# Final state products of three head groups made inside the second norm, with their operands parked in DRAM

## The chip, the cores and the metric

The kernel runs on one core of a Trainium2 chip. The core has a matrix engine (PE, with its weight loads shown as PEld), a vector engine (DVE), an activation engine (ACT), a general engine (POOL) and a queue engine (SP) that here only issues transfers. Matrix products read SBUF and write to PSUM; POOL works on SBUF tiles. The metric is device time in microseconds for one execution of the whole program. Three runs of the kernel before gave 1777.72, 1773.81 and 1773.94 us, a median of 1773.94 us.

## The reference

One inference step of a decoder layer with 256 prompt tokens and 8 x 8 sample tokens (320 columns together), all in float32. The layer has a mixing part and a feed-forward part, each between two root-mean-square norms:

```
h = rms_norm(x);  proj = h @ w_in            # u, v | z | x, B, C | dt
mix = concat(chunk_gate(u, v), ssd(z, x, B, C, dt)) @ w_out
x = x + rms_norm(mix)                        # the "second norm"
f = gelu(g) * u of causal_conv(rms_norm(x) @ w_up);  x = x + rms_norm(f @ w_down)
```

The part the change touches is the state-space mixer (SSD). It has 32 heads in 4 groups of 8 heads; a group shares B and C. The prompt is cut in two chunks of 128 tokens. For a group, the state after the prompt is

```
states[c]  = B[c]^T (decay[c] * dt * x)[c]               # 128 x 512 for a group, one per chunk c
final      = chunk_decay * states[0] + states[1]         # returned as ssm_state_prompt
```

`states[0]` is needed for the outputs of the second chunk. `states[1]` is needed by nothing but `final`, which is only an output.

## The kernel before

Activations are kept transposed: features on the 128 partitions, 320 tokens along the free axis. Each large float32 product with weights is made from three reduced-precision products: weights and activations are split in a rounded high part and a remainder (`whi`, `wlo` and `h_hi`, `h_lo`), and high x high, high x low and low x high are accumulated (lines 153 to 155). Weights come in slabs of 128 x 1024 elements: SP loads `wraw`, ACT casts it to `whi` (L124), DVE subtracts to get `wlo` (L125), with three buffers of each.

The order of work is traced by Python code, and a planner then places each instruction: on each engine it takes, of the instructions that are ready in its own estimate, the one of highest priority; the priority is the place in the trace unless a block raises it (`first()` and `high_priority`). Tiles of one tag share a fixed number of buffers, and a new tile waits until an old one's last reader is done. `issue_after(ins)` orders those instructions of a block that run on the engine of `ins` behind `ins` in that engine's queue; instructions of the block on other engines are not ordered by it. Background tasks are Python generators in the list `bg`; the projection loops call `tick()` between slabs, which advances the first task by one step.

The mixer's second half runs four tasks `ssd(g)`, one per head group, while projections and output products fill PE. In a group: `xt_ps` transposes of x; `xdt` = dt * x; `x0d` = the decayed first chunk (POOL, L851, tag `xde`, two buffers); `s1_ps` = the product for `states[0]` (L897), copied by ACT to `s1` (L899, one buffer); the states of the samples (`up_ps`, `yo_ps`); decays of each head (`cs`, three buffers); the output products `y_ps` (L1004). At the end of the group `x1d`, the decayed second chunk (L851 again), is ready, POOL multiplies `s1` by the chunk decay (L1027), and `final()` (L1030 to L1036) makes the product `fin_ps` of `btok` and `x1d` (L1032), DVE adds it to `s1` (L1034), and a queue stores the result (L1035). For groups 0 to 2 this happens in the task itself after two more steps. For group 3 `final()` is kept in `rest` and its two halves are run in the second norm.

The second norm ends the mixing part. Its order is written out by hand: after the last output product, the last sample states of group 3 (`rest[0]`), the column sums of squares on PE (`tsum`, L294), the product `fin_ps` of group 3, the root (ACT, L282, recorded in `rooted`) and a Newton step on DVE (L283 to L286), then `spread` (L302), three PE transposes that leave 1/rms of every token in a PSUM bank, `r2b`. DVE reads that bank for the scaled residual (`x1_ready`: L1141, L1142), ACT makes the high part of the next norm's input (L401), DVE the low part (L402; its instruction is recorded in `low`), and the up projection starts. PE has no work of its own between `tsum` and the first product of the up projection. `idle_products` (L817) puts products there whose result nobody reads: one ahead of `spread` and seven behind it.

PSUM has eight banks: four of tag `mm` for projections and four of tag `ms` for everything else (`misc`). The first part of the up projection uses four `mm` banks and two `ms` banks; `r2b` holds a third `ms` bank until its last reader.

Of the kernel before, what the change touches and what calls it, by code (L numbers as in the profile page):

```python
# [9 lines left out]
F32 = mybir.dt.float32  # L10
# [3 lines left out]
ALU = mybir.AluOpType  # L14
# [3 lines left out]
P = 128  # L18
# [3 lines left out]
NT = NP + NS  # L22
# [12 lines left out]
def hybrid_step(  # L35
# [10 lines left out]
    act, dve, pool, pe, sp = nc.scalar, nc.vector, nc.gpsimd, nc.tensor, nc.sync  # L46
# [4 lines left out]
    dr = ctx.enter_context(tc.tile_pool(name="dr", bufs=1, space=DRAM))  # L51
# [5 lines left out]
    def misc(name):  # L57
        return ms.tile([P, 512], F32, tag="ms", name=name)
# [6 lines left out]
    with tc.high_priority(offset=300000):  # L65
        dve.memset(ones, 1.0)

        ps = misc("early")
# [202 lines left out]
    rsqrt_ins, sums_ins, spread_ins, rooted, low = [], [], [], [], []  # L271
# [17 lines left out]
    def token_sums(*sqs):  # L289

        ps = misc("tsum")
        for c, o in enumerate((0, P, NT - P)):
            for i, sq in enumerate(sqs):
                ins = pe.matmul(ps[:, c:c + 1], sq[:, o:o + P], ones[:, 0:1], start=i == 0, stop=i == len(sqs) - 1).ins  # L294
        sums_ins.append(ins)
        return ps[:, 0:3]
# [40 lines left out]
    def squares_of(total):  # L337

        one, held = [], []

        def step(nb):
            if nb < KD - 3:
                add_square(total, acc[:, nb, :], nb == 0)
                if nb == 0:

                    act.activation(tp.tile([P, 1], F32, name="root_there", bufs=1), total[:, 0:1], AF.Sqrt)
                return
            with first():
                if nb < KD - 1:
                    held.append(misc("sq_ps")[:, :NT])  # L350
                else:
                    one.append(tp.tile([P, NT], F32, tag="sq", name="sq", bufs=2))
                for ts in parts_of(nb):
                    act.activation((one or held)[-1][:, ts], acc[:, nb, ts], AF.Square)
                if nb > KD - 3:
                    dve.tensor_tensor(out=total, in0=total, in1=held.pop(0), op=ALU.add)
        return step, one


    dacs_d = dr.tile([NH, NT + NS], F32, name="dacs_d")  # L360
    tot_d = dr.tile([NH, NB], F32, name="tot_d")
    ssq_d = [dr.tile([P, NT // 32], F32, name=f"ssq_d{i}") for i in range(4)]


# [56 lines left out]
    with ExitStack() as mctx:  # L421
        op = mctx.enter_context(tc.tile_pool(name="op", bufs=1))
# [365 lines left out]
        with tc.tile_pool(name="sd", bufs=1) as sd:  # L788
# [23 lines left out]
            x_of = {0: x0}  # L812
            rest = []

            def idle_products(ps, n):
                for _ in range(n):
                    ins = pe.matmul(ps, bsp[:, 0, :P], bsp[:, 0, :], start=True, stop=True).ins  # L817
                return ins

            def ssd(g):  # L820

                xs = x_of[g]
# [125 lines left out]
                def end(i, by=act):  # L948
                    made = grown(sts[i], bms.pop(i))
                    store_state(i, sts[i], by)  # L950
                    return made
# [75 lines left out]
                pool.tensor_tensor(out=by_head(s1), in0=by_head(s1),  # L1027
                                   in1=dec[:, 2, h0:h0 + 8].unsqueeze(2).to_broadcast([P, 8, 64]), op=ALU.mult)

                def final():  # L1030
                    ps = misc("fin_ps")
                    made = pe.matmul(ps, btok[:, 1, bs], x1d, start=True, stop=True)  # L1032
                    yield made.ins
                    dve.tensor_tensor(out=s1, in0=s1, in1=ps, op=ALU.add)  # L1034
                    (pool if g == 3 else act).dma_start(o_ssm_p[g], s1)  # L1035
                    yield  # L1036
                if g == 3:
                    rest.extend([lambda: end(3, pool), final()])
                else:
                    yield  # L1040
                    yield
                    for _ in final():
                        pass

            tasks = [ssd(g) for g in range(4)]
            res = [[] for _ in range(4)]
# [50 lines left out]
            finish(norm3)  # L1097
            sq2 = hp.tile([P, NT], F32, tag="ssq", name="sq2")

            squares, one = squares_of(sq2)  # L1100
            chunk_out(w_out, 7, *res[3], False, squares, apart=True)

# [4 lines left out]
            with first():  # L1107
                with tc.issue_after(pd_last[-1]), tc.issue_after(added_last[0]):
                    made = rest[0]()
                with tc.issue_after(made):  # L1110
                    most = token_sums(sq2)
                with tc.issue_after(sums_ins[-1]):
                    ps = token_sums(*one)
                with tc.issue_after(sums_ins[-1]):
                    made = next(rest[1])
                r = rsqrt_by_root(most, ps, 1.0 / D)
                behind = rsqrt_ins[-1]

                idle = misc("idle")
                with tc.issue_after(made):  # L1120
                    made = idle_products(idle, 1)
                with tc.issue_after(made):
                    r2b = spread(r)
                with tc.issue_after(spread_ins[-1]):
                    idle_products(idle, 7)
            sq3 = hp.tile([P, NT], F32, tag="ssq", name="sq3")


# [18 lines left out]
            load_x(1)  # L1147
            up0 = []
            project(ffn_w_up, 0, None, late=up0, ready=x1_ready, after=behind, ahead=1, more=DFF, held=added)
            with tc.issue_after(low[2]):  # L1150
                next(rest[1])

            room = [op.tile([P, 4, NT], F32, tag="xs", name="sq_two", bufs=2) for _ in range(2)]
            total, *some = [t[:, i:i + 2, :] for t in room for i in (0, 2)]
# [281 lines left out]
```

## Time and profile before

| | |
|---|---|
| three runs | 1777.72, 1773.81, 1773.94 us; median 1773.94 us |
| profiled execution | 1774.69 us; span on the core 1773.0 us |
| granted TensorE clock | 0.999 of full |
| busy: PE, DVE, ACT, POOL | 1765.1, 1173.7, 817.9, 274.5 us |
| DMA | 290.01 MB, mean 164 GB/s |

The span is the time from the first to the last instruction of the core; 1.7 us of the execution lie outside it. A row of a timeline gives start, duration, engine, line, operation and operands, in us from the span's start; a bracket at its end gives the engine's idle time before it and what released it. The view of waits gives total, number and longest. A group's row gives shortest, median and longest duration in ns. The chain of work that ended last is followed back from the last instruction, so its pieces do not overlap and a piece on it is time that the program took.

### The profile page before, as it was taken

The numbers are of one execution on the slowest core, as the hardware profiler recorded it, in microseconds if no ns is written. First come the engines' busy times: TensorE is split into PE (matmuls) and PEld (weight loads), VectorE is DVE, ScalarE is ACT, GpSimd is POOL, SyncE is SP. The second block draws the span as 40 slices with busy tenths as digits, with TensorE's granted clock in tenths as the row PEclk, the third lists the DMA queues.
The fourth block names the chain that finished last, engine by engine and source line by source line (L and its number), as shares of the span: only waits on it lengthen the run. The fifth ranks groups of instructions, "written<-read, shape, count | busy, mean of one in ns | idle before, by whom it ended". The sixth has DMA issues, their size and how long they took to land.

```text
span 1773.0 us, 30633 instructions
## 1 busy us (share of the span) xinstructions
PE 1765.1 (100%) x11897; PEld 1711.9 (97%) x11897; DVE 1173.7 (66%) x2015; ACT 817.9 (46%) x1193; POOL 274.5 (15%) x602
## 2 busy tenths in 40 slices
PE   9999999999999999999999999999999999999998
PEld 7789999999999998999999999999999999999998
DVE  7549764657978778678865465656657575656575
ACT  5434555334564556445645334343434343333445
POOL 1202200000331313103211011010102010101004
PEclk9999999999999999999999999999999999999999
DMA  7556645455666666555554554555455544454542
GB/s 261 161 150 171 189 141 159 153 152 182 223 189 195 186 203 188 147 179 158 171 158 147 154 153 148 155 148 153 150 151 158 144 156 145 156 155 145 155 151 102
DMA packets 217297, 290.01 MB, mean 164 GB/s; under 512 B 19264, under 2 KB 146624, under 8 KB 216960
## 3 DMA queue, kind: packets, MB, share of 16 engines
q1 hardware_dynamic: 205424, 268.84, 50.1%
q10 hardware_dynamic: 10016, 14.16, 2.2%
q0 software_dynamic: 1712, 5.05, 1.0%
q8 instruction: 94, 1.54, 0.4%
q14 instruction: 51, 0.42, 0.1%
HBM read 273.17 MB, written 14.84 MB: 162 GB/s over the span
## 4 chain that ended last, share of the span: by engine, by line
PE 98%; DVE 1%; issue 0%; ACT 0%; ACTq 0%; DVEq 0%
PE ps L153 19%; PE ps L154 19%; PE ps L155 19%; PE pd L153 10%; PE pd L155 10%; PE pd L154 10%; PE ps_v L144 7%; PE y_ps L1004 1%; PE up_ps L925 0%; PE sg L752 0%; PE yo_ps L908 0%; PE xt_ps L414 0%; PE early L70 0%; PE x1p L1299 0%; DVE xsp L863 0%
## 5 line engine op out<-in xcount | busy, mean ns | idle before, releaser
L125 DVE TENSOR_TENSOR wlo<-wraw,whi 128x1024 fp32r<-128x1024 f32 (+1 forms) x476 | 582.3, 1223 | 421.4 <-ACT whi L124 419.6
L124 ACT CAST whi<-wraw 128x1024 fp32r<-128x1024 f32 (+1 forms) x475 | 495.1, 1042 | 714.5 <-PE ps L154 381.5
L153 PE MATMUL ps<-h_hi,whi 128*128 128x320 f32 x2268 | 700.6, 309 | 0.0
L154 PE MATMUL ps<-h_lo,whi 128*128 128x320 f32 x2268 | 699.3, 308 | 0.0
L155 PE MATMUL ps<-h_hi,wlo 128*128 128x320 f32 x2268 | 698.9, 309 | 0.0
L153 PEld LDWEIGHTS ps<-h_hi,whi 128*128 128x128 f32 x2268 | 425.7, 188 | 2.5 <-issue 1.6
L154 PEld LDWEIGHTS ps<-h_lo,whi 128*128 128x128 f32 x2268 | 425.8, 188 | 0.7
L155 PEld LDWEIGHTS ps<-h_hi,wlo 128*128 128x128 f32 x2268 | 425.6, 188 | 0.0
L155 PE MATMUL pd<-fhi,wlo 128*128 128x320 f32 x704 | 217.0, 308 | 0.0
L153 PE MATMUL pd<-fhi,whi 128*128 128x320 f32 x704 | 217.0, 308 | 0.0
L154 PE MATMUL pd<-flo,whi 128*128 128x320 f32 x704 | 217.0, 308 | 0.0
L153 PE MATMUL pd<-ohi,whi 128*128 128x320 f32 x448 | 139.1, 310 | 0.0
L155 PE MATMUL pd<-ohi,wlo 128*128 128x320 f32 x448 | 138.4, 309 | 0.0
L154 PE MATMUL pd<-olo,whi 128*128 128x320 f32 x448 | 138.1, 308 | 0.0
L153 PEld LDWEIGHTS pd<-fhi,whi 128*128 128x128 f32 x704 | 132.2, 188 | 0.0
L154 PEld LDWEIGHTS pd<-flo,whi 128*128 128x128 f32 x704 | 132.2, 188 | 0.0
L155 PEld LDWEIGHTS pd<-fhi,wlo 128*128 128x128 f32 x704 | 132.2, 188 | 0.0
L1201 POOL COPY ptf<-pad 128x2 f32<-128x2 f32 x88 | 21.0, 238 | 602.7 <-DVE pad L1189 601.9
L249 DVE TENSOR_TENSOR acc_ffn<-acc_ffn,pd 128x320 f32<-128x320 f32 (+1 forms) x161 | 77.5, 482 | 37.8 <-PE pd L155 36.3
L153 PEld LDWEIGHTS pd<-ohi,whi 128*128 128x128 f32 x448 | 84.1, 188 | 1.6 <-issue 1.0
L154 PEld LDWEIGHTS pd<-olo,whi 128*128 128x128 f32 x448 | 84.1, 188 | 0.3
L155 PEld LDWEIGHTS pd<-ohi,wlo 128*128 128x128 f32 x448 | 84.1, 188 | 0.2 <-issue 0.2
(335 smaller groups left out, 1866.5 us busy)
## 6 DMA issues: line engine op xcount, KB each, us to landing
wraw<-in_ffn_w_up SPq DMA_DIRECT2D x176, 512.0 KB, 3.6
wraw<-in_w_in SPq DMA_DIRECT2D x140, 512.0 KB, 3.8
wraw<-in_ffn_w_down SPq DMA_DIRECT2D x88, 512.0 KB, 3.3
wraw<-in_w_out SPq DMA_DIRECT2D x64, 512.0 KB, 3.4
st<-in_state_ssm SPq DMA_DIRECT2D x32, 256.0 KB, 4.1
out_ssm_state_sample<-st ACTq DMA_DIRECT2D x30, 256.0 KB, 4.1
cs<-dacs_d SPq DMA_DIRECT2D x16, 320.0 KB, 4.7
xr<-in_xT SPq DMA_DIRECT2D x4, 640.0 KB, 4.0
```

Of the source, the lines that this page charges most:

```text
L124: rounded[:] = [act.copy(hi, raw).ins]
L125: dve.tensor_tensor(out=lo, in0=raw, in1=hi.bitcast(F32), op=ALU.subtract)
L144: made = pe.matmul(out, xi, w[g][wi], start=first and begins, stop=last and ends)
L153: pe.matmul(ps, whi, xhi, start=first, stop=False)
L154: pe.matmul(ps, whi, xlo, start=False, stop=False)
L155: return pe.matmul(ps, wlo, xhi, start=False, stop=last).ins
L249: added_last[:] = [dve.tensor_tensor(out=acc[:, nb, ts], in0=acc[:, nb, ts], in1=ps[:, ts], op=ALU.add).ins]
L1004: pe.matmul(ps[64 * i:64 * i + 64, cols], w(hl), x(hl, m, cpx), tile_position=(0, 64 * i), **flags)
L1201: pool.tensor_copy(ptf[:, k, :], pad[:, 256:258])
```

## The change

The unread products are gone, with their helper. A task `ssd(g)` of groups 0 to 2 no longer makes its final product: it stores the scaled `s1` and the operand `x1d` to two new DRAM tiles from POOL's queue, and ends there, without the two further steps. Group 3 keeps both in SBUF. `load_ends()`, traced ahead of the last output chunk, loads the six parked tiles back on SP's queue: the three `s1` into the buffer of tag `xdt`, the three `x1d` into the three buffers of tag `cs`. In the second norm the four products are made in this order: group 3 where it was; group 0 ahead of `spread` where the single unread product was; groups 1 and 2 behind `spread` where the seven were. The second half of `final` is no longer a DVE add out of PSUM: ACT copies the bank to SBUF (over `x1d`), POOL adds it to `s1`, and POOL's queue stores it. For groups 3 and 0 this second half stands behind the root on ACT, for groups 1 and 2 it is traced after the up projection's first part.

```diff
+    s1_d, x1_d = ([dr.tile([P, 512], F32, name=f"{n}_d{g}") for g in range(3)] for n in ("s1", "x1"))
...
-            def idle_products(ps, n):
-                for _ in range(n):
-                    ins = pe.matmul(ps, bsp[:, 0, :P], bsp[:, 0, :], start=True, stop=True).ins
-                return ins
...
-                def final():
-                    ps = misc("fin_ps")
-                    made = pe.matmul(ps, btok[:, 1, bs], x1d, start=True, stop=True)
-                    yield made.ins
-                    dve.tensor_tensor(out=s1, in0=s1, in1=ps, op=ALU.add)
-                    (pool if g == 3 else act).dma_start(o_ssm_p[g], s1)
-                    yield
                 if g == 3:
-                    rest.extend([lambda: end(3, pool), final()])
+                    at_end[g] = s1, x1d
+                    rest.append(lambda: end(3, pool))
                 else:
-                    yield
-                    yield
-                    for _ in final():
-                        pass
+                    pool.dma_start(s1_d[g], s1)
+                    pool.dma_start(x1_d[g], x1d)
+
+            at_end = {}
+
+            def load_ends():
+                s1s = sd.tile([P, 3, 512], F32, tag="xdt", name="s1s", bufs=1)
+                for g in range(3):
+                    x1 = sd.tile([P, 2, NT], F32, tag="cs", name="x1s", bufs=3).rearrange("p i n -> p (i n)")[:, :512]
+                    sp.dma_start(x1, x1_d[g])
+                    sp.dma_start(s1s[:, g], s1_d[g])
+                    at_end[g] = s1s[:, g], x1
+
+            def final(g):
+                ps = misc("fin_ps")
+                s1, x1d = at_end[g]
+                yield pe.matmul(ps, btok[:, 1, P * g:P * g + P], x1d, start=True, stop=True).ins
+                act.copy(x1d, ps)
+                pool.tensor_tensor(out=s1, in0=s1, in1=x1d, op=ALU.add)
+                pool.dma_start(o_ssm_p[g], s1)
+                yield
...
+            load_ends()
             squares, one = squares_of(sq2)
             chunk_out(w_out, 7, *res[3], False, squares, apart=True)
...
+                ends = [final(g) for g in range(4)]
                 with tc.issue_after(sums_ins[-1]):
-                    made = next(rest[1])
+                    made = next(ends[3])
                 r = rsqrt_by_root(most, ps, 1.0 / D)
                 behind = rsqrt_ins[-1]
-
-                idle = misc("idle")
+                with tc.issue_after(rooted[-1]):
+                    next(ends[3])
                 with tc.issue_after(made):
-                    made = idle_products(idle, 1)
+                    made = next(ends[0])
+                with tc.issue_after(rooted[-1]):
+                    next(ends[0])
                 with tc.issue_after(made):
                     r2b = spread(r)
-                with tc.issue_after(spread_ins[-1]):
-                    idle_products(idle, 7)
+                for g in (1, 2):
+                    with tc.issue_after(spread_ins[-1]):
+                        next(ends[g])
...
             project(ffn_w_up, 0, None, late=up0, ready=x1_ready, after=behind, ahead=1, more=DFF, held=added)
-            with tc.issue_after(low[2]):
-                next(rest[1])
+            for g in (1, 2):
+                with tc.issue_after(low[g]):
+                    next(ends[g])
```

## The prediction

> **What bounds the kernel now.** I read the page first, then PE's waits, then the chain around the old products, then the norm's timeline.
>
> ```profile
> span 1773.0 us, 30633 instructions
> PE 1765.1 (100%) x11897; PEld 1711.9 (97%) x11897; DVE 1173.7 (66%) x2015; ACT 817.9 (46%) x1193; POOL 274.5 (15%) x602
> ```
> ```profile
> PE early L70 <- DVE ones L66: 1.1, 1, 1.1
> PE spread L302 <- DVE rs_r L286: 0.7, 2, 0.4
> PE up_ps L925 <- DVE xsp L863: 0.5, 2, 0.2
> PE ps L190 <- ACT h_hi L401: 0.2, 1, 0.2
> ```
>
> PE is busy for all but 8 us, and the waits that the trace names come to 2.5 us. So work taken out of PE's dense stream is time won, and any new wait of PE is time lost. The chain at the first of the three group ends:
>
> ```profile
> 497.81 1.69 PE y_ps L1004 x32
> 503.24 0.86 PE fin_ps L1032 x2
> 504.10 0.87 PE xt_ps L414 x8
> 509.84 0.86 PE s_ps L897 x2
> 594.84 0.86 PE fin_ps L1032 x2
> 683.42 0.86 PE fin_ps L1032 x2
> ```
>
> One final product is two passes, 0.86 us on the chain, at each of the three ends. Now the second norm, PE then ACT then DVE:
>
> ```profile
> 821.30 1.10 PE L1032 MATMUL fin_ps<-xde,btok 128*128 128x512 f32 x2
> 821.84 0.80 PE L817 MATMUL idle<-bsp 128*128 128x512 f32 x1
> 823.06 0.51 PE L302 MATMUL spread<-ident,rs_r 128*128 128x128 f32 x3 [0.42 <-DVE rs_r L286]
> 823.33 1.85 PE L817 MATMUL idle<-bsp 128*128 128x512 f32 x7
> 825.34 0.41 PE L190 MATMUL ps<-h_hi,whi 128*128 128x320 f32 x1 [0.16 <-ACT h_hi L401]
> ```
> ```profile
> 821.91 0.20 ACT L282 ACTIVATE rs_s<-rs_v 128x3 f32<-128x3 f32 x1 [1.18 <-DVE rs_v L281]
> 822.02 1.03 ACT L124 CAST whi<-wraw 128x1024 fp32r<-128x1024 f32 x1
> 824.72 0.56 ACT L401 ACTIVATE h_hi<-acc_mix,prm 128x320 fp32r<-128x320 f32 x1 [1.67 <-DVE acc_mix L1142]
> 826.04 0.56 ACT L401 ACTIVATE h_hi<-acc_mix,prm 128x320 fp32r<-128x320 f32 x1 [0.76 <-DVE acc_mix L1142]
> ```
> ```profile
> 823.61 0.55 DVE L1141 SCALAR_TENSOR_TENSOR acc_mix<-acc_mix,prm,spread 128x320 f32<-128x320 f32 x1 [0.70 <-PE spread L302]
> 824.19 0.49 DVE L1142 TENSOR_TENSOR acc_mix<-acc_mix,xr 128x320 f32<-128x320 f32 x1
> ```
>
> The hole's length is set by the chain root, Newton step, spread, L1141, L1142, h_hi, first product at 825.34; not by the products in it. Behind the hole DVE is as full as PE, and POOL is empty:
>
> ```profile
> core 0: us, PE busy (x) PEld busy (x) DVE busy (x) ACT busy (x) POOL busy (x), PEclk, DMA share, GB/s
> 825.50:841.50 16.00, 16.00 (x110) 16.00 (x111) 16.00 (x31) 8.54 (x13) 0.00 (x0) 1.00 0.52 155
> ```
>
> **The change, part by part.**
>
> Three products leave the dense stream: 3 x 0.86 = 2.58 us gained. Their three DVE adds out of PSUM leave with them; DVE is no bound there, so they count nothing.
>
> In the hole PE has room for them. Group 3's product occupies PE from 821.30 for 0.86, to 822.16; group 0's follows to 823.02, and the spread started at 823.06. Groups 1 and 2 start where the seven stood, 823.33, and need 1.72, to 825.05, against 825.34. Group 2's needs a PSUM bank: four are shared by `r2b` and three earlier products, so it waits for ACT's copy of group 3's. If ACT does the cast of 822.02 first, that copy is done at about 822.11 + 1.03 + 0.58 = 823.7 (length from the row below), and group 2's product would start at 823.33 + 0.86 = 824.19. So PE pays 0 here. The unread products filled PE where it had no work; the new ones fill the same stretch, 2.58 in place of eight short products, so the granted clock (1.00 in the row of 825.50 above) has no longer idle time to react to.
>
> ACT gets four copies of a 128x512 bank. `issue_after(low[g])` names a DVE instruction and the second half has none on DVE, so it orders nothing: the copies go where ACT has room. Rows for a copy, a POOL operation of this size, and POOL's queue:
>
> ```profile
> L899 ACT COPY s<-s_ps x4: 578/580/580, 441.6 to 691.4; 128x512 f32<-128x512 f32 x4
> L851 POOL TENSOR_TENSOR xde<-xdt,dec x8: 1041/1044/1489, 439.0 to 695.8; 128x512 f32<-128x512 f32 x8
> L1035 POOL DMA_DIRECT2D out_ssm_state_prompt<-s x1: 542/542/542, 855.5 to 855.5; - x1
> out_ssm_state_prompt<-s POOLq DMA_DIRECT2D x1, 256.0 KB, 4.9
> ```
>
> ACT's idle 1.67 ahead of 824.72 holds two copies (1.16) and the 0.76 ahead of 826.04 a third. Between 0 (all fit) and 0.58 (one stands in front of an h_hi); I take 0.2, nearer to the first since the gaps fit.
>
> POOL gets four adds with both inputs in SBUF, each 1.04 or more, into a stretch where POOL did nothing and DVE is full. The trace shows what such a meeting costs:
>
> ```profile
> L993 DVE TENSOR_TENSOR cs<-cs,cb_cms x32: 473/484/1351, 444.6 to 730.3; 128x320 f32<-128x320 f32 x32
> 499.25 1.79 DVE L125 TENSOR_TENSOR wlo<-wraw,whi 128x1024 fp32r<-128x1024 f32 x1
> 500.95 0.54 DVE L1014 SCALAR_TENSOR_TENSOR xs<-xs,prm,y_ps 128x320 f32<-128x320 f32 x1
> 499.91 2.02 POOL L1027 TENSOR_TENSOR s<-s,dec 128x512 f32<-128x512 f32 x1
> L335 POOL TENSOR_TENSOR sq<-sq,sq x24: 877/889/1860, 798.1 to 1752.0; 128x320 f32<-128x320 f32 x24
> 838.32 1.22 DVE L125 TENSOR_TENSOR wlo<-wraw,whi 128x1024 fp32r<-128x1024 f32 x1
> ```
>
> While POOL worked from 499.91 the subtraction took 1.79 instead of 1.22 (0.57 more) and POOL's operation 2.02 instead of 1.04; L1014, which reads a PSUM bank, kept its 0.54; L993, two SBUF inputs, reaches 1.35 from 0.48 (0.87 more). L335 stretches to 1.86 from 0.88. So the two engines hinder each other where DVE reads two SBUF tiles; that is L1142, L402 and L125 here, and not L1141. Each add costs DVE between 0 (it falls under L1141, or POOL is the one that waits) and 0.87; I take 0.6, nearest to the 0.57 that the operation of the same width cost: 4 x 0.6 = 2.4.
>
> The Trainium skill ("SBUF — State Buffer", Who interferes with whom) says that a DVE instruction with two SBUF inputs and a GpSimd instruction that reads SBUF exclude each other for the whole instruction, whichever issues first. The rows agree with the exclusion; by that rule alone, were POOL always first, each add would cost its full length instead of my 0.6, which is the third rival.
>
> How much of DVE's delay reaches PE? The slack between DVE's result and PE's use of it:
>
> ```profile
> 828.57 1.01 DVE L402 SCALAR_TENSOR_TENSOR h_lo<-acc_mix,prm,h_hi 128x320 fp32r<-128x320 f32 x2
> 829.99 0.19 PEld L154 LDWEIGHTS ps<-h_lo,whi 128*128 128x128 f32 x1
> 840.26 0.19 PEld L155 LDWEIGHTS ps<-h_hi,wlo 128*128 128x128 f32 x1
> ```
>
> L402's pair ends at 829.58 and PE loads with it in flight at 829.99, 0.4 later; the subtraction of 838.32 ends at 839.54 and is used at 840.26, 0.7 later. DVE has no gap in between to catch up, so delays add up and only about 0.4 is absorbed, once: 2.4 - 0.4 = 2.0 lost. Bounds 0 and 4 x 0.87 = 3.5.
>
> At the group ends the next group starts earlier: its first transposes follow `y_ps` at 499.50 instead of 504.10, so 4.6 us sooner. The new queue work is POOL's: two stores, 0.54 each to issue. Behind them on POOL stands the next `x0d`, and `s1`, one buffer, is free only when its store has landed: 499.91 + 2.02 + 0.54 + 4.9 = 507.4. The ACT copy that needs it:
>
> ```profile
> 512.00 0.58 ACT L899 COPY s<-s_ps 128x512 f32<-128x512 f32 x1
> ```
>
> moves from 512.00 to 507.4 at the earliest. That just meets; what is queued behind it on ACT are casts. The upper bound of a start: `x0d`, and with it `s_ps`, late by a stretched POOL operation (2.02 - 1.04) and the two issues ahead of it (1.08), 2.1 us; the lower, a little below 0, since the steps at an end are no longer bunched with the next start's. I take 0.1 in all, near 0, because `s_ps` comes 5.7 us behind the first transposes (504.10 to 509.84) and keeps that distance. `x1d` depends on nothing of the group's end, so its store can go early and its buffer is free in time. The six loads (256 KB each) are traced a whole output chunk ahead of their use and go through SP's queue between slab loads. They cost between 0 and one landing, 4.9, if a slab came late by it; I take 0, as PE's waits above name no load at all.
>
> Sum: -2.58 + 0.2 + 2.0 + 0.1 = -0.3 us. On the profiled execution 1774.69 becomes 1774.4; that execution is 0.75 above the median, so against the median 1773.94 the forecast is 1773.7 us.
>
> **The rivals.**
>
> First: the adds are free. Falling under L1141 or waiting themselves, they delay no DVE operation, and all of the gain stays: -2.58 + 0.2 + 0.1, 1771.7 us. For it: L335's 1.86 shows that POOL is often the one that waits. Against it: DVE's 16.00 of 16.00 and the 0.57.
>
> Second, on the other side: the early start of the next group. If `s1`'s store lands later than 507.4, or the next `xdt` is late because DVE is still with L125 and L1014 until 501.5, PE's `s_ps` and ACT's casts wait. At 1.5 us for each of three starts, three quarters of the 2.1 above, it is 4.5 more: 1778.1 us. It decides the sign from 0.2 us a start, and would pass 0.3% only near two. Against it: PE waited only 0.5 in all in this region so far, and it has projection work to do.
>
> Third: each add takes the port ahead of DVE and holds it throughout, 4 x 1.04 - 0.4 = 3.8 instead of 2.0: 1775.5 us, slower by 1.5. It decides from 0.7 us an add. For it: L993's 0.87. Against it: four times in a row is unlikely, since every block of the stretch has its L1141, under which POOL may work freely.
>
> Fourth: the change does not place the last two second halves as it says. The copies wait until late, like the old add out of PSUM:
>
> ```profile
> 854.55 0.68 DVE L1034 TENSOR_TENSOR s<-s,fin_ps 128x512 f32<-128x512 f32 x1
> ```
>
> Then two adds fall past the full stretch and cost nothing: 4 x 0.6 becomes 2 x 0.6, 1772.5 us.
>
> **How the numbers follow.** Forecast 0.42 (1772.8 to 1774.9), free adds 0.2, early start 0.13, port lost each time 0.15, late copies 0.07, something unseen 0.03. The range 1771.4 to 1776.6 takes in all but most of the early start and a little below the free adds. A measurement of this kernel tells about 0.3%, 5.3 us, from no change. Faster by more would need twice the work that is removed: 0.03. Slower by more needs eight us of new waits, the far part of the early start and the unseen: 0.09. Within: 0.88.
>
> **What would show it.** Right: no `fin_ps` on the chain at group ends; four of them between `tsum` and the first up product, that product 0.3 to 1 us later against the last `tsum`; POOL busy at 4 us or more behind the hole; L1142, L402 or L125 with maxima well over 0.48, 0.55 and 1.22 there, and PE waiting some 2 us in all on DVE results. Wrong: PE waiting on `s_ps` or casts at the starts of groups, `fin_ps` waiting for a bank, or DVE's durations unchanged.

## The result: 6.4 us longer

| | before | after |
|---|---|---|
| median of six runs each | 1775.13 us | 1781.55 us |
| lowest and highest | 1773.81 to 1777.72 | 1778.79 to 1785.27 |
| profiled execution | 1774.69 us | 1778.79 us |
| its span, granted clock | 1773.0 us, 0.999 | 1777.1 us, 0.999 |

The ratio is 1.0034, with a 95% interval of 1.0019 to 1.0048. The six runs of before include the three from which the prediction's 1773.94 was taken. The prediction was 1773.7 us, 1771.4 to 1776.6: wrong in size and in sign, and outside its range. The profiled execution of after is the shortest of its six, so its trace can explain 4.1 us; the other five have no trace. The three runs of after below 1781 us had a granted clock of 0.999, the three above 1783 us 0.997 or 0.998, so a part of the 6.4 us is probably lost clock; where it was lost isn't recorded.

Span and busy times on the page of after:

```profile
span 1777.1 us, 30650 instructions
PE 1764.7 (99%) x11889; PEld 1710.6 (96%) x11889; DVE 1178.5 (66%) x2011; ACT 823.9 (46%) x1201; POOL 283.5 (16%) x615
```

PE is busy for 0.4 us less than before and the span is 4.1 us longer. So PE waits. PE's waits in after (us in total, times, longest):

```profile
PE cb_ps L873 <- DVE xs L1010: 2.0, 1, 2.0
PE up_ps L921 <- DVE xsp L859: 1.8, 2, 1.0
PE ps L154 <- DVE h_lo L403: 1.6, 1, 1.6
...
PE ps L190 <- DVE h_lo L403: 0.4, 1, 0.4
```

Two lines stand at the starts of head groups (`cb_ps`, `up_ps`, 3.8 us together, where the only such wait before was 0.5), two behind the hole of the second norm (`h_lo`, 2.0 us, which were not there). To see what each place took, compare three marks of PE's timeline: `tsum`, the first product of the up projection (L190), and the first product of the next part (`ps_one`). After:

```profile
821.92 1.39 PE L294 MATMUL tsum<-ones,sq 128*128 128x1 f32 x12
827.46 0.85 PE L190 MATMUL ps<-h_hi,whi 128*128 128x320 f32 x4 [0.28 <-ACT h_hi L402]
872.40 0.31 PE L153 MATMUL ps_one<-h_hi,whi 128*128 128x320 f32 x1
```

and before, whose L190 stood at 825.34:

```profile
820.04 1.39 PE L294 MATMUL tsum<-ones,sq 128*128 128x1 f32 x12
867.68 0.31 PE L153 MATMUL ps_one<-h_hi,whi 128*128 128x320 f32 x1
```

- Up to `tsum`: 1.88 us later, although three products of 0.86 us are gone. Against the 2.58 us that their absence was to save, the mixer's half is 1.88 + 2.58 = 4.46 us worse.
- The hole, `tsum` to L190: 5.54 against 5.30 us, 0.24 longer.
- The stretch behind it, L190 to `ps_one`: 44.94 against 42.34 us, 2.60 longer.
- From there to the end of the span, code that the change does not touch: 904.70 against 905.32 us, 0.62 shorter.

Together 4.1 us. The first place in the view by windows (columns: length, then busy time of PE, its weight loads, DVE, ACT and POOL with their instructions, granted clock, DMA share, GB/s), first before, then after:

```profile
430.00:800.00 370.00, 369.39 (x2678) 349.29 (x2677) 291.28 (x506) 208.44 (x377) 85.55 (x104) 1.00 0.61 191
```
```profile
430.00:800.00 370.00, 365.99 (x2659) 346.32 (x2658) 292.33 (x501) 211.53 (x379) 87.85 (x109) 1.00 0.63 197
```

PE stood idle for 0.61 us of these 370 before and for 4.01 after: 3.40 of the 4.46 us, at a full clock. The other 1.06 us are not seen as waits. Where group 2 ends and group 3 starts, after, by DVE, POOL and PE:

```profile
672.08 2.06 DVE L125 TENSOR_TENSOR wlo<-wraw,whi 128x1024 fp32r<-128x1024 f32 x1
674.07 1.03 DVE L449 SCALAR_TENSOR_TENSOR cv<-pad,prm,cv 128x344 f32<-128x344 f32 x1
675.02 0.53 DVE L1010 SCALAR_TENSOR_TENSOR xs<-xs,prm,y_ps 128x320 f32<-128x320 f32 x1
```
```profile
671.68 1.38 POOL L1023 TENSOR_TENSOR s<-s,dec 128x512 f32<-128x512 f32 x1 [4.47 <-PE y_ps L1000]
673.96 0.76 POOL L980 TENSOR_TENSOR cpx<-cpx,cT 128x256 f32<-128x256 f32 x1
```
```profile
675.61 0.71 PE L873 MATMUL cb_ps<-cT,bT 128*128 128x128 f32 x4 [2.00 <-DVE xs L1010]
```

L1010 is the last step of group 2's output (L1014 before). It stands behind a subtraction that POOL's L1023 stretched from 1.22 to 2.06 us and behind L449, a step of the convolution for the next heads, which took 1.03 instead of 0.57 beside POOL's L980. PE waits 2.00 us for it. Before, the convolution had ended by then: DVE's time on its tile `cv` between 672 and 686 us, before and then after:

```profile
672.00:686.00 14.00, 0.00 (x0) 1.00 0.56 163
```
```profile
672.00:686.00 14.00, 2.32 (x4) 1.00 0.47 155
```

ACT shows the same meeting. In these rows it loads a table where it changes between the convolution's function and the group's. The two groups of ACT's table loads between 430 and 790 us that changed, before and then after (columns: number, busy us and ns of one, idle us before them):

```profile
L453 ACT ACT_TABLE_LOAD x2 | 2.6, 1283 | 0.0
L991 ACT ACT_TABLE_LOAD x1 | 1.3, 1283 | 0.0
```
```profile
L454 ACT ACT_TABLE_LOAD x4 | 5.1, 1283 | 1.5 <-DVE cv L449 1.4
...
L987 ACT ACT_TABLE_LOAD x3 | 3.8, 1283 | 0.1
```

At the lines of the convolution (L453, now L454) and of the decays (L991, now L987) three loads came to be seven; with the two groups that did not change, ten became 14. The second place, behind the hole in after, by PE, POOL and DVE:

```profile
824.12 1.02 PE L1046 MATMUL fin_ps<-x1s,btok 128*128 128x512 f32 x2
...
825.30 1.88 PE L1046 MATMUL fin_ps<-x1s,btok 128*128 128x512 f32 x4
829.30 0.85 PE L190 MATMUL ps<-h_lo,whi 128*128 128x320 f32 x4 [0.41 <-DVE h_lo L403]
832.23 0.42 PE L154 MATMUL ps<-h_lo,whi 128*128 128x320 f32 x1 [1.63 <-DVE h_lo L403]
```
```profile
827.13 1.29 POOL L1048 TENSOR_TENSOR s1s<-s1s,x1s 128x512 f32<-128x512 f32 x1
829.30 2.52 POOL L1048 TENSOR_TENSOR s1s<-s1s,x1s 128x512 f32<-128x512 f32 x2
```
```profile
827.45 1.34 DVE L1154 TENSOR_TENSOR acc_mix<-acc_mix,xr 128x320 f32<-128x320 f32 x1
829.63 2.55 DVE L403 SCALAR_TENSOR_TENSOR h_lo<-acc_mix,prm,h_hi 128x320 fp32r<-128x320 f32 x1
```

The four products fit the hole as planned. The first of POOL's four adds, at 824.99, held next to nothing. Its add of 827.13 held DVE's L1154 for 0.86 us (1.34 against 0.48), and the two adds that follow each other from 829.30 held one L403 for 2.00 (2.55 against 0.55). That is 2.86 us of DVE, and PE's 2.60.

### The profile page after: what moved, and what is told of

The parts are those of the page before. It is cut to its first block, busy times and chain, and to the rows that moved or that the text cites. A ratio compares the mean times of both kernels' runs of the same rounds, so it can differ in the third digit from the quotient of the medians.

```text
span 1777.1 us, 30650 instructions
## 1 busy us (share of the span) xinstructions
PE 1764.7 (99%) x11889; PEld 1710.6 (96%) x11889; DVE 1178.5 (66%) x2011; ACT 823.9 (46%) x1201; POOL 283.5 (16%) x615
## 4 chain that ended last, share of the span: by engine, by line
PE 94%; DVE 3%; DMA 1%; ACT 1%; issue 1%; SPq 0%; DVEq 0%; ACTq 0%
PE ps L153 18%; PE ps L154 18%; PE ps L155 18%; PE pd L153 10%; PE pd L154 10%; PE pd L155 10%; PE ps_v L144 7%; DVE wlo L125 1%; PE y_ps L1000 1%; DMA cs<-dacs_d 0%; PE up_ps L921 0%; PE sg L753 0%; PE yo_ps L904 0%; DVE cv L449 0%; DMA st<-in_state_ssm 0%
## 5 line engine op out<-in xcount | busy, mean ns | idle before, releaser
L125 DVE TENSOR_TENSOR wlo<-wraw,whi 128x1024 fp32r<-128x1024 f32 (+1 forms) x476 | 584.2, 1228 | 423.5 <-ACT whi L124 421.5
```

The costliest lines, as they stand in the source:

```text
L125: dve.tensor_tensor(out=lo, in0=raw, in1=hi.bitcast(F32), op=ALU.subtract)
```

## The experiments

All ratios are to runs of the kernel before that were measured together with the run. A ratio is estimated from all the runs and is not the quotient of the medians, which for e1 and e3 is larger (1.0048 and 1.0031). "PE idle" is 370 us less PE's busy time between 430 and 800 us in the profiled execution. It is one trace each: the edit of e4 lies behind these 370 us and PE's products ahead of it come in the same order as before, and yet its PE idle is 0.89 us more and its `tsum` comes 1.44 us later (821.48). So differences of about a microsecond between two traces show nothing here.

| run | median us | ratio to before, interval | PE idle us |
|---|---|---|---|
| after | 1781.55 | 1.0034 [1.0019, 1.0048] | 4.01 |
| after, adds on DVE (e2) | 1778.82 | 1.0019 [1.0010, 1.0028] | 3.28 |
| after, steps put back (e1) | 1783.19 | 1.0035 [1.0023, 1.0048] | 2.96 |
| after, both (e3) | 1780.21 | 1.0020 [1.0011, 1.0030] | 6.07 |
| e3, parking stores on ACT's queue (e8) | 1777.76 | 1.0014 [1.0006, 1.0023] | 4.28 |
| before, no unread products (e4) | 1776.62 | 1.0008 [0.9999, 1.0017] | 1.50 |
| before, no steps at three ends (e5) | 1781.13 | 1.0035 [1.0023, 1.0047] | 8.35 |
| before, no steps at ends 0 and 1 (e13) | 1780.18 | 1.0033 [1.0021, 1.0045] | 3.39 |
| before, no steps at end 2 (e12) | 1775.87 | 1.0004 [0.9995, 1.0013] | 1.15 |
| before, four steps (e11) | 1778.19 | 1.0012 [1.0003, 1.0020] | 3.79 |
| before, with the parking stores (e6) | 1775.74 | 1.0003 [0.9994, 1.0012] | 2.11 |
| before, no products at three ends (e9) | 1775.16 | 1.0004 [0.9995, 1.0013] | 2.35 |
| e9 with the parking stores (e10) | 1776.33 | 1.0007 [0.9998, 1.0016] | 3.69 |

### The adds behind the hole

e2 makes the four adds on DVE, from the SBUF copy, late in the first part of the up projection:

```diff
-                pool.tensor_tensor(out=s1, in0=s1, in1=x1d, op=ALU.add)
+                yield
+                dve.tensor_tensor(out=s1, in0=s1, in1=x1d, op=ALU.add)
...
+            for g in (3, 0, 1, 2):
+                with tc.issue_after(low[13]):
+                    next(ends[g])
```

> The changed kernel, with the four adds made by DVE behind the last blocks of the residual instead of by POOL during them. Theory A (POOL's adds hold up DVE where it is full, and PE behind it): DVE's longest L403 and L1154 go back to 0.55 and 0.49 us, PE's waits on h_lo (2.0 us) vanish, and the span falls by about 2.5 us to 1774.6. Theory B (PE waits there for another reason, the four ACT copies in front of h_hi): the waits on h_lo stay, 1 us or more, and the span stays above 1776.

The median came to 1778.82 us, 2.7 under after, though the intervals of the two ratios overlap. The trace is clearer. Its `tsum` and `ps_one`:

```profile
821.62 1.40 PE L294 MATMUL tsum<-ones,sq 128*128 128x1 f32 x12
869.51 0.31 PE L153 MATMUL ps_one<-h_hi,whi 128*128 128x320 f32 x1
```

From one to the other are 47.89 us, where after took 50.48 and before 47.64, no wait of PE on `h_lo` is left, and no L403 takes more than 0.55 us, while ACT's copies are still there. So POOL's adds cost 2.6 us, as the first theory said. The rest of the loss, 1778.82 against 1774.65 before, stays.

### The start of the next group

e5 changes only the order of tracing: the kernel before, without the two empty steps at the ends of groups 0 to 2.

```diff
                 else:
-                    yield
-                    yield
                     for _ in final():
                         pass
```

> The kernel before, with one thing changed: the two empty steps ahead of the final product of groups 0 to 2 are gone, so the next group starts as early as in the changed kernel; products, adds and stores stay. Theory A (the early start alone costs): PE's waits on cb_ps and up_ps appear as in the changed kernel, and the median is 2 us or more above the kernel before. Theory B (what is taken away or added around the ends costs, not the start): within 1 us of the kernel before.

It ran for 1781.13 us, 6.0 more than before (1775.1), at a clock of 0.999 to 1.000 in each run. Its trace is of the longest of its six runs, 1783.17 us. Its largest waits of PE, and the place of the first one by DVE and PE:

```profile
PE xt_ps L414 <- DVE xs L1014: 2.9, 1, 2.9
PE up_ps L925 <- DVE xsp L863: 2.7, 3, 1.3
PE yo_ps L908 <- DMA st<-in_state_ssm: 1.2, 1, 1.2
```
```profile
677.57 2.01 DVE L448 SCALAR_TENSOR_TENSOR cv<-pad,prm,cv 128x344 f32<-128x344 f32 x2
...
680.38 1.22 DVE L125 TENSOR_TENSOR wlo<-wraw,whi 128x1024 fp32r<-128x1024 f32 x1
681.52 1.04 DVE L448 SCALAR_TENSOR_TENSOR cv<-pad,prm,cv 128x344 f32<-128x344 f32 x1
682.48 0.54 DVE L1014 SCALAR_TENSOR_TENSOR xs<-xs,prm,y_ps 128x320 f32<-128x320 f32 x1
```
```profile
683.07 0.44 PE L414 MATMUL xt_ps<-ident,xs 128*128 128x128 f32 x2 [2.88 <-DVE xs L1014]
```

It is the picture of after, as the first theory said, though PE's wait on `xs` stands at `xt_ps` and not at `cb_ps`; and none of the change's products, stores or adds are there: the last output step of group 2 stands behind the convolution of the next heads, and ACT loads 14 tables. Removing the two steps is enough to cost about what the whole change cost (1.0035 against 1.0034). That it is the only cause in after isn't shown by this: see the steps put back, below.

Which of the three ends does it? e12 takes the steps out at the end of group 2, as in the diff; e13, with `g == 2` as the condition, at the ends of groups 0 and 1.

```diff
-                    yield
-                    yield
+                    if g < 2:
+                        yield
+                        yield
```

> The kernel before with the two empty steps ahead of the final product taken out at the end of group 2 only; groups 0 and 1 keep theirs. Theory C (an early start costs because the steps saved at the ends add up and push the first half of a later group's output into the convolution of the next heads, where DVE and ACT switch between the two kinds of work): the convolution of the last heads is over when group 2 ends, so nothing collides; 10 table loads on ACT between 430 and 790 us as before, no PE wait on xs above 0.5 us, 1775 to 1776.5 us. Theory S (each start made early costs about a third of the 6.0 us that the three cost together, as its own DVE chain is late): about 1777 us, with PE waits of 1 to 2 us behind the end of group 2.

> The kernel before with the two empty steps taken out at the ends of groups 0 and 1, and kept at the end of group 2. Theory C (the saved steps add up and meet the convolution of the later heads): nearly the whole cost of the three, 1780 to 1782 us, with 13 or 14 table loads on ACT between 430 and 790 us, and convolution work on DVE between the last output product of group 2 and the group's xs. Theory S (a third for each start): about 1779 us, waits spread over the two starts.

e12 gave 1775.87 us, 1.1 above before, with an interval that includes no change; e13 gave 1780.18, 5.4 above. So the cost comes with the first two ends, as the first theory said of the time. e13 has 14 table loads and, between 672 and 690 us, 5.01 us of convolution on DVE where before and e12 have none. But its waits of PE stand elsewhere:

```profile
PE up_ps L925 <- DVE xsp L863: 1.8, 3, 1.3
PE yo_ps L908 <- DMA st<-in_state_ssm: 1.4, 1, 1.4
```

They are at the starts of groups 1 and 2 themselves, as the second theory said, not at the meeting with the convolution. The steps saved at ends 0 and 1 therefore set the cost and do push later work into the convolution, but how much of the 5.4 us is that meeting, and how much the earlier starts finding DVE and a state's transfer late, these runs don't divide. In after and in e5 the largest wait is at the meeting, in e13 none is.

e11 goes the other way, with four steps instead of two.

```diff
                     yield
                     yield
+                    yield
+                    yield
```

> The kernel before with four empty steps ahead of the final product at the ends of groups 0 to 2 instead of two; nothing else is changed. Theory A (DVE's backlog sets when the next group can start; an earlier start cost 6.0 us): a later start finds DVE free, so PE waits at the starts of 0.5 us or less, and a time within 1 us of before, 1774 to 1776. Theory B (the place is tuned, and any other alignment of POOL's operations with the subtractions costs about as much): 1778 to 1782 us, with new waits of PE of 2 us or more in all on DVE's results at the starts.

At 1778.19 us against 1775.74 it lost 2.4 us. Its largest wait of PE is of another kind:

```profile
PE y_ps L1004 <- issue: 1.6, 1, 1.6
```

A later start finds DVE free (`up_ps` waits 0.5 as before) and is late with its own decays and outputs: beside this line PE waits 0.8 us each on a state's transfer and on `cs`. In the 4 us behind the wait of 1.6 us, from 592 us on, the granted clock is 0.57, another 1.7 us of full speed lost in this trace. So the first theory, that a later start would do, falls. The time is that of the second, but its waits on DVE come to 1.3 us instead of 2 or more.

### The products taken out, and the stores put in

e9 is the kernel before without the three products and their adds; the steps stay.

```diff
-                    for _ in final():
-                        pass
+                    act.dma_start(o_ssm_p[g], s1)
```

> The kernel before, without the three final products and their adds for groups 0 to 2: what is stored there is the scaled first state alone, so three of the four prompt states lack their second part. Nothing is parked, the steps stay. If the 2.58 us of the three products are PE's time and nothing else changes, the median falls by 2.58. Theory B2 (without the product the next start meets DVE and POOL otherwise, and the stretch of the subtractions eats the gain): within 1 us of the kernel before or slower, with PE's waits on up_ps above 2 us.

1775.16 us against 1775.1: nothing gained, though PE has 2.58 us less to do. The interval, 0.9 us shorter to 2.3 longer, leaves no room for a gain of 2.58. PE's largest wait:

```profile
PE up_ps L925 <- DVE xsp L863: 1.8, 3, 1.3
```

It was 0.5 us before. Half of the time freed at the ends is seen again in this wait on DVE's `xsp`. PE's idle time in the half is 2.35 against 0.61 us, but e4 shows 1.50 with this half unchanged, so where the rest went isn't shown.

e6 is the kernel before with the six parking stores on POOL's queue, e10 is e9 with them.

```diff
+                    pool.dma_start(s1_d[g], s1)
+                    pool.dma_start(x1_d[g], x1d)
```

> The kernel before, with the six parking stores on POOL's queue added and nothing else (their contents are not read, and all products stay). Theory B1 (two issues of 0.58 us on POOL at each end push POOL's x0d and the states' products against DVE's two-input operations): the subtractions at the starts stretch, PE waits on up_ps, median 2 us or more above the kernel before. Theory B2 (it is the removal of the product and of DVE's add that moves the starts): within 1 us of the kernel before.

> The kernel before, with the three products and DVE adds of groups 0 to 2 taken out and the six parking stores put on POOL's queue; the two steps and the unread products stay, nothing is loaded back, and three of the four prompt states are stored without their second part. Taking out the products alone gave 1775.16 us against 1775.1 before, the stores alone 1775.74. Theory M (the stores and the missing product do harm together: with nothing between the end of a group and the next, the stores on POOL's queue shift POOL's products onto DVE's subtractions at the next start): 1777 to 1780 us, PE waits on xsp above 2.4 us as in the two kernels with the steps put back. Theory N (each is harmless, so what stays lost in those two kernels comes from the hole, from the loads or from the end of the layer's half): 1775 to 1776.3 us, waits on xsp at 1.8 us or less.

e6 came to 1775.74 us, 0.6 over the 1775.1 of before, and e10 to 1776.33, also 0.6 over the runs of before measured with it (1775.74); both intervals include no change. The stores cost little, as the second theory of e6 said, alone or together with the missing products. e10's `up_ps` did wait 3.2 us for `xsp`, which was expected of the harm of both together, but its time is below what that theory asked for: neither expectation is met in full.

### Putting the steps back

If the missing steps are the fault, after should mend when they return. e1 puts them behind the parking stores of after, e3 does that and moves the adds to DVE as e2 does, e8 is e3 with the six stores on ACT's queue.

```diff
                     pool.dma_start(s1_d[g], s1)
                     pool.dma_start(x1_d[g], x1d)
+                    yield
+                    yield
```

> The changed kernel, with the two empty steps put back behind the stores at the end of groups 0 to 2, so that the next group starts where it did in the kernel before. Theory A (the early start of the next group made PE wait, 4.4 us of the changed kernel's profile between 430 and 790 us): the waits of PE on cb_ps and up_ps at the starts fall back to about 0.5 us in all, and the profile's span is 4 us or so below the 1777.1 of the changed kernel, near 1773. Theory B (it is the parking itself, the stores and loads, that costs): the waits stay and the span is within 1 us of 1777. The stretch behind the second norm should stay as in the changed kernel: PE still waits some 2 us on h_lo.

> Both of the other two edits together. If the two causes are separate and there is no third, both savings come: the span is 4 + 2.5 below 1777.1, about 1770.6, that is some 2.4 us below the kernel before, which is the 2.58 of the three products less the copies. If the products in the hole or the stores have a cost of their own, it stays above 1772. In the times, a median that lies further from the profile than in the kernel before would speak for a third cause, a clock that is granted less in some executions.

> The changed kernel with the steps put back, the adds on DVE, and the parking stores issued from ACT's queue instead of POOL's. Theory B1 (POOL's issues cost): PE's waits on up_ps fall below 1 us, the profile's span is below 1772 and the median below the kernel before. Theory B2: like the same kernel with POOL's stores, median 4 us or more above the kernel before.

They gave 1783.19, 1780.21 and 1777.76 us: the steps alone mend nothing in the median, and even the best of the three is over before by 0.0006 to 0.0023 of its time. No expectation is met in full: e1's waits on `up_ps` are 2.6 us where 0.5 was expected, e3's span is 1779.8 instead of 1770.6, and e8 still waits 3.6 us on `up_ps` but lost 2.7 us, not 4. ACT's table loads are back at ten in all three, so the meeting with the convolution is gone. Another has come. e1, DVE, POOL and PE in group 3:

```profile
696.25 2.10 DVE L125 TENSOR_TENSOR wlo<-wraw,whi 128x1024 fp32r<-128x1024 f32 x1
698.28 0.67 DVE L923 TENSOR_TENSOR st<-st,up_ps 128x512 f32<-128x512 f32 x1
698.98 0.69 DVE L859 TENSOR_TENSOR xsp<-xq,xsp 64x512 fp32r<-64x512 f32 x1
```
```profile
694.94 2.33 POOL L915 TENSOR_TENSOR st<-st,tote 128x512 f32<-128x512 f32 x2
```
```profile
699.82 0.76 PE L921 MATMUL up_ps<-xsp,bm 128*128 128x512 f32 x1 [2.38 <-DVE xsp L859]
```

The first of POOL's two operations ends at 696.25, where the subtraction starts; the second holds it (2.10 against 1.22 us), `xsp` comes late, and PE waits 2.38. The windows of e1 around it:

```profile
696.00:700.00 4.00, 1.62 (x11) 1.39 (x11) 3.94 (x5) 0.62 (x1) 1.27 (x2) 0.97 0.15 22
700.00:704.00 4.00, 4.00 (x20) 2.68 (x20) 2.47 (x6) 1.65 (x3) 0.71 (x1) 0.60 0.74 244
```

In the four microseconds behind it the clock granted to PE is 0.60, 1.6 us of full speed lost. e3 has the same wait at 705.90 us with a clock of 0.66 from 708 to 712. That such a wait makes the kernel lose more clock in all isn't shown: the trace of before loses as much near its end, from 1759.45 to 1762.86 us at 0.50, where e1's loses none. e3's shortest run, 1774.65 us, is as short as before, and its longest, 1781.91, is not; the shorter runs of e3 had a clock of 0.999, those above 1779 us 0.997 or 0.998. That the spread is lost clock fits these numbers, but only profiled runs show where it is lost, and e3's profiled run lost some more at 244 to 252 us, ahead of everything that the change touches. Why e1's other four runs are 3.6 us and more above its profiled one stays open, and so does what keeps e3 and e8 above before once the steps are back and the adds are gone from POOL.

### The unread products

e4 is the kernel before without the eight unread products and with nothing in their place.

```diff
-                with tc.issue_after(made):
-                    made = idle_products(idle, 1)
...
-                with tc.issue_after(spread_ins[-1]):
-                    idle_products(idle, 7)
```

> The kernel before without its eight unread products, and nothing in their place: PE is idle from the end of the product of group 3 to the spread and from there to the first up product. Theory A (the unread products only fill idle time): within 1 us of the kernel before. Theory C (they keep the clock granted, and the times of the changed kernel scatter because its hole or its waits lose it in some executions): slower than the kernel before by 2 us or more, with a lower mean granted clock, in some executions or all.

1776.62 us against 1774.65, 2.0 more, with an interval of the ratio that just includes one. That is at the edge of what the second theory asked for, and no more than that. The windows of its profiled execution show a lost clock:

```profile
825.00:830.00 5.00, 3.31 (x12) 3.31 (x13) 4.97 (x12) 1.94 (x4) 0.00 (x0) 0.50 0.08 28
830.00:835.00 5.00, 5.00 (x30) 5.00 (x30) 3.84 (x9) 2.17 (x4) 0.00 (x0) 0.82 0.50 150
```

With the hole empty the clock falls to 0.50 and then 0.82: 2.5 + 0.9 = 3.4 us of full speed, part of it while PE waits anyway. In after the same stretch keeps 1.00. In these traces the four products did the work of the eight in this respect, and the time lost behind the hole in after is no clock.

## Why the prediction was wrong, step by step

- **The products taken out (-2.58 us).** Failed as a gain by itself. "So work taken out of PE's dense stream is time won" holds while PE is the engine that comes last; at the start of a group DVE comes last by a little, so the sentence "DVE is no bound there" fails there too. e9 took exactly this work out and gained nothing measurable.
- **The group ends (0.1 us).** This is the step that failed most: for -2.58 + 0.1 in the mixer's half, after's trace has +1.88. It kept `s_ps` 5.7 us behind the first transposes and that was right: in after `s_ps` did move earlier with its start. But the time was not set by `s_ps`. The term asked what the start itself would wait for, and not what the saved steps do to the tasks traced behind it: the first half of a later group's output moved, and with it came the convolution, four more table loads, and waits on `xs` and `xsp`. Without anything else of the change it cost 6.0 us (e5), and the first two ends alone 5.4 (e13). That it accounts for all of the loss in after isn't shown, since putting the steps back did not bring the time back (e1, e3, e8).
- **The second rival** named the early start and the right sign, at a chance of 0.13, and gave 4.5 us for what measured 6.0. Its first condition, a late store of `s1`, did not come about; its second, DVE being late with L125 and L1014, did, but PE then waited in `cb_ps` and `up_ps`, not in `s_ps`. That its bound of 2.1 us a start, 6.3 in all, would have held the 6.0 is luck: it was built from a stretched operation and two issues of POOL, and the issues cost little (e6). The sign turned from 0.13 us a start, (0.28 + 0.1) / 3, and not from 0.2.
- **The adds on POOL (2.0 us).** Right in mechanism, place and sign: L1142's and L402's counterparts were held, PE waited on `h_lo`, and e2 confirmed it. The size was short: one add held nothing, one 0.86 us, and two in a row 2.00, a mean of 0.72 for each instead of 0.6. Of these 2.86 us 0.26 were absorbed, where 0.4 was taken. Measured 2.6. Each POOL add was also longer than in the row used, 1.27 to 1.30 us instead of 1.04. And the 0.57 was read beside the wrong operation. This row of before stands just ahead of the two that the prediction compared:

```profile
499.22 0.73 POOL L984 TENSOR_TENSOR cpx<-cpx,cT 128x256 f32<-128x256 f32 x1 [7.28 <-ACT cpx L983]
```

It began 0.03 us ahead of the subtraction of 499.25 and can explain its 0.57, while L1027, which began during the subtraction, is the one that grew, to 2.02. So 0.57 was what an operation of 0.73 us cost when it came first, and no price for one of 128x512. L993's 0.87, taken as the bound, is nearer to what an add that held DVE cost, 0.86 and twice 1.00.

- **The third rival** saw an add holding DVE throughout and judged a run of such losses unlikely because L1141 lies between. Two adds back to back did not let DVE come between them, and L1141 was of no help there.
- **The copies on ACT (0.2 us)** went early into ACT's gaps, and the hole grew by 0.24. Right. The fourth rival, late copies, did not happen.
- **PSUM banks, loads and stores (0).** No wait of PE on a bank or on the six loads is seen, and the stores alone moved the time by 0.6 us, within the interval. Right.
- **The clock.** That the four products would hold it in the hole was right; that it could be lost behind short waits elsewhere was not considered.

The parts measured one by one give 6.0 for the steps and 2.6 for the adds, 8.6 against 6.4 for the whole. The difference of 2.2 lies within the intervals (e5's alone goes from 4.1 to 8.3 us), so it shows no gain elsewhere. Nor do the two parts explain everything: with both put right, e3 and e8 are still 5.6 and 2.7 us above before by their medians. What sets that rest stays open. In e8 and in e10, which both lack the products at the ends, keep the steps and park the operands, PE waits about as long on `xsp` at the start of group 2 (3.10 and 2.70 us), but e10 is only 0.6 us above before.

## What to carry to other kernels

In this kernel a step of a background task was also a delay for every task behind it: before taking steps out, follow where the later tasks land, and count what they share with the work there (DVE's queue, ACT's tables), not only what the next instruction waits for. Work taken off the busiest engine is a gain only where that engine comes last in that stage; taking it out alone, in a version that computes less, tests that. When work goes to POOL beside a full DVE, price each operation by which engine starts first, and by whether it stands alone or follows another of POOL's directly. Here moving the adds to DVE, later on, won the 2.6 us back; gaps between them on POOL were not tried.

## What the runs showed of the hardware that was not expected

- Two POOL operations that follow each other can hold one DVE operation with two SBUF inputs through both: 2.55 instead of 0.55 us at L403 in after. The Trainium skill ("SBUF — State Buffer", Who interferes with whom) gives the lock for one instruction; here DVE did not get in between two.
- A wait of PE of 2.38 us was followed by a granted clock of 0.60 over 4 us (e1), and one of 1.63 us by 0.57 (e11), but one of 2.88 us in e5 by no loss:

```profile
680.00:684.00 4.00, 1.12 (x9) 0.93 (x8) 4.00 (x7) 2.81 (x6) 1.72 (x1) 1.00 0.77 256
684.00:688.00 4.00, 4.00 (x32) 3.81 (x31) 3.69 (x8) 2.78 (x5) 1.04 (x1) 1.00 0.32 117
```

The Trainium skill ("TensorE: Matmul & The Clock Gate", Why this matters for your kernels) advises against idle gaps of PE above about 3 us; those of e1 and e11 were shorter and lost clock all the same. In e3 the clock is 0.50 in two stretches of 3.41 us, from 246.54 and from 707.34 us. Their starts lie 460.80 us apart, 135 times 3.4133, which agrees with the same page's window (What's actually happening) of 3413 ns that does not start anew with the kernel. So it can depend on where in that window a wait falls, but how idle PE must be in one isn't shown: in the 3.41 us ahead of the half clock PE was busy for 1.07 us in e1, 1.78 in e11, 2.37 in e3 (ahead of 246.54) and 2.98 in the kernel before (ahead of 1759.45), while 1.92 and 2.03 us in the two such windows around e5's wait (678.27 to 685.10) lost none.
